# A decoder block in fp32 products: four pairs instead of three by seven products in three down groups of each FFN

## The chip, the core and the metric

The kernel runs on one core of one Trainium2 chip. The metric is the device time of the whole program in microseconds. The engines are named as the profile names them: PE is the matrix engine and PEld its weight loads, DVE the vector engine, ACT the scalar engine, POOL the GpSimd engine, SP the engine that issues most DMAs.

## What is computed

One layer of a hybrid decoder block on 256 tokens of width 2048: a half-step SwiGLU FFN, a mixer (gated DeltaNet beside stick-breaking attention), a second half-step FFN and an input embedding. The change touches the two FFNs:

```python
def swiglu(x, w_gu, w_down):
    gate, up = jnp.split(x @ w_gu, 2, axis=-1)
    return (jax.nn.silu(gate) * up) @ w_down
...
h = h + 0.5 * swiglu(rms_norm(h, ffn1_norm[i]), ffn1_w_gu[i], ffn1_w_down[i])
```

The hidden width is 5632, eleven blocks of 512.

## The kernel before

**Splits.** Every float32 matrix is split into a rounded part and its residue (`hi`, `lo`). A product of two such matrices takes three matmuls of 128 x 128 by 128 x 512: hi by hi, hi by lo and lo by hi. ACT makes `hi` with a copy that rounds, DVE makes `lo` with a subtraction.

**Pairs and groups.** Weights come in *pairs*: 256 rows by 512 columns, of 0.5 MB. `weight_pair` (L66 to L79) loads one on SP's queue into one of four `raw` tiles and splits it (L77 on ACT, L78 on DVE). A *group* makes four banks of the accumulator memory (PSUM): two column blocks `b` by two token halves. A gate/up group makes one block of gate and one of up. A down group makes two column blocks of the result; `nb` is 0 for a part's first down group and 2 for its second. A pair taken *plain* (L541 to L552) costs 12 matmuls for one column block.

**Parts.** The eleven hidden blocks are made in three parts, `PARTS` = (0 to 2), (3 to 6), (7 to 10). Within a part come the gate/up groups of its blocks, then the two down groups, which use those blocks as the left side.

**Seven products.** The first `ns` pairs of a group aren't taken plain. Seen over both column blocks and both row halves of a pair, they are a 2 by 2 product of blocks, done with seven products instead of eight (Winograd's form of Strassen's scheme). `NS` is 4 for gate/up groups. `NS_DOWN` is 2 in part one and 3 in parts two and three. One product is 3 x `ns` matmuls (`product`, L321 to L352). In the order `SEVEN` = 0, 1, 2, 4, 3, 5, 6, products 0, 4 and 6 use blocks of the left side as they are (A11, A12 and A22), the others use sums of them, the *left sides* `Sh` and `Sl`.

**The right sides.** The four quarters of the weights (row half by column block) are loaded whole into four R tiles (L279), for most groups on POOL's queue. `all_sums` (L289 to L327) makes the seven right sides one after the other: a copy that rounds on ACT (`shi`, L298) and a residue on DVE (`slo`, L299), each in two buffers. Between them a quarter is changed in place. `add` does it on DVE (L307). `add_loaded` does it with an accumulating DMA from POOL's queue, which reads the second operand from HBM again (L314). Before the change B11 + B12, right after the first product's right side, is an `add`; B12 + B22 and the last sum are `add_loaded`.

**Who comes when.** `plan` (L355) writes the order out by hand. While a group's plain pairs run, the seven products of the *next* group (its follower) are put between them: `at` says behind which plain pair. The first three quarters of the group after that are loaded behind products five to seven, the last one behind the first plain pair of the group that follows. `next_weights` (L88) makes pairs and right sides up to two or three ahead of use. A scheduler then orders each engine's instructions by this sequence and by what it expects to be ready. `tc.keep_in_program_order` pins one instruction to the place where it was written.

**Left sides.** `halves` (L423) makes them: DVE adds hi and lo back together (L456), forms four sums in place (L462), ACT rounds (L464), DVE takes the residue (L465). For the down groups of parts two and three it is started behind the sixth product of the part's last gate/up group (L536 to L539), with `at_once` = 1, one pair at a time. It runs as a *lane*: `lanes.step` after every plain pair takes it one `yield` further. The scheduler needs `Sh` free, of which there is one buffer.

**From gate/up to down.** `down_input` (L479) is a lane too. DVE multiplies (L482) and transposes in blocks (`tb`, L487), four DMAs write to HBM (`scr`, L493), one DMA reads back (`tT`, L498), and some steps later ACT and DVE split the block into `hTh` and `hTl` (L504, L505). `tb` and `tT` share one buffer. For a part's last block the DMAs go by SP's queue and the split stands `last` steps behind `tT`'s DMA: 3 for parts of four blocks, 2 for part one. `Group` sorts a first down group's plain pairs so that those of the last block come last.

**The tag `nat`** is a ring of four tiles of 128 x 512 floats. The copies `part` of partial products (L349) use it, and so do the left-side tiles here.

## Time and profile before

| | us |
|---|---|
| device time, median of 3 runs | 1944.5 (1944.01 to 1945.11) |
| the profiled execution | 1945.28 |
| its span in the profile | 1943.6 |
| FFN one, part two: last gate/up group, first and second down group | 341.0 to 377.2, to 418.7, to 464.9 |
| the other three places of the same kind begin near | 587, 1484 and 1730 |

The profile's times count from the start of the span. A line such as `L299 DVE TENSOR_TENSOR slo<-R,shi 128x1536 ...` names the line of the kernel, the engine, the operation, output and inputs, then count, total busy time and mean length in ns, then the time for which that engine was idle just before, and what ended it. A row of windows gives start and end, the length, and then for PE, PEld, DVE, ACT and POOL the busy time with the number of instructions, the granted PE clock, the DMA engines' share and GB/s. A row of the timeline gives start and length in us. In a row of waits stand the total, the number and the longest. Matmuls are pipelined: one begins before the one before it ends, so their lengths add up to more than the time they take.

### The profile page before, as it was taken

The page shows a single profiled execution, that of the slowest core. Times are in us where ns is not written, and L with a number is a line of the kernel's source. Part 1 is how long each engine was busy: PE and PEld are TensorE (multiplying, and loading weights), DVE is VectorE, ACT ScalarE, POOL GpSimd, SP SyncE. Part 2 cuts the span into 40 slices and gives each one's busy share as a digit, 9 for nine tenths or more (in the row PEclk, how much of TensorE's full clock was granted, in tenths as well). Part 3 has the DMA queues.
Part 4 walks back from the last instruction along what each step waited for, and adds up shares of the span by engine and source line. Part 5 has one row for each costly group of instructions (what it writes and reads, how often), then busy time and mean ns, then how long its engine had stood idle before and what let it go on. Part 6 is the DMA issues. An engine that isn't in the chain of part 4 may idle for free.

```text
span 1943.6 us, 24163 instructions
## 1 busy us (share of the span) xinstructions
PE 1928.1 (99%) x8884; PEld 1594.0 (82%) x8884; DVE 1570.4 (81%) x1703; ACT 1164.1 (60%) x1362; POOL 148.4 (8%) x226
## 2 busy tenths in 40 slices
PE   9999999999999999999999999999999999999998
PEld 7888888888888888878788888888888888888886
DVE  7879878997789766797856579899888987888865
ACT  6656666666666557664555456566556755657654
POOL 0010110000010000010100000010000100001000
PEclk9999999999999999999999999999999999999999
DMA  8778898888888765556565776788888987989764
GB/s 307 269 236 282 252 293 285 237 288 249 280 285 242 228 218 171 176 169 211 161 213 159 244 283 231 226 281 289 248 275 241 327 264 244 271 237 314 234 214 143
DMA packets 144182, 475.05 MB, mean 244 GB/s; under 512 B 19648, under 2 KB 47296, under 8 KB 129856
## 3 DMA queue, kind: packets, MB, share of 16 engines
q1 hardware_dynamic: 107200, 302.16, 44.4%
q0 software_dynamic: 25920, 160.44, 30.2%
q10 hardware_dynamic: 10944, 10.91, 1.8%
q8 instruction: 69, 1.13, 0.2%
q14 instruction: 49, 0.40, 0.1%
HBM read 451.44 MB, written 22.02 MB: 244 GB/s over the span
## 4 chain that ended last, share of the span: by engine, by line
PE 92%; DVE 5%; DMA 2%; issue 1%; ACT 0%; POOL 0%; SPq 0%; POOLq 0%; DVEq 0%; ACTq 0%
PE d L550 5%; PE d L552 5%; PE d L551 5%; PE u L551 5%; PE u L552 5%; PE u L550 5%; PE g L343 5%; PE g L342 5%; PE g L344 5%; PE g L551 4%; PE g L552 4%; PE pj L112 4%; PE pj L113 4%; PE pj L114 4%; PE g L550 4%; PE d L344 3%
## 5 line engine op out<-in xcount | busy, mean ns | idle before, releaser
L77 ACT CAST whi<-raw 128x1024 fp32r<-128x1024 f32 (+1 forms) x489 | 511.3, 1049 | 401.1 <-PE pj L114 106.6
L78 DVE TENSOR_TENSOR wlo<-raw,whi 128x1024 fp32r<-128x1024 f32 (+1 forms) x489 | 592.0, 1218 | 162.9 <-ACT whi L77 161.8
L299 DVE TENSOR_TENSOR slo<-R,shi 128x2048 fp32r<-128x2048 f32 (+2 forms) x224 | 444.9, 1989 | 132.1 <-ACT shi L298 130.1
L298 ACT CAST shi<-R 128x2048 fp32r<-128x2048 f32 (+2 forms) x224 | 373.9, 1671 | 141.5 <-DVE R L307 62.7
L112 PE MATMUL pj<-whi,nTh 128*128 128x512 f32 x448 | 179.4, 401 | 0.0
L113 PE MATMUL pj<-wlo,nTh 128*128 128x512 f32 x448 | 175.2, 391 | 1.1 <-DVE wlo L78 1.1
L114 PE MATMUL pj<-whi,nTl 128*128 128x512 f32 x448 | 174.9, 390 | 0.0
L550 PE MATMUL d<-whi,hTh 128*128 128x512 f32 x448 | 174.5, 390 | 0.0
L551 PE MATMUL d<-wlo,hTh 128*128 128x512 f32 x448 | 174.4, 389 | 0.0
L552 PE MATMUL d<-whi,hTl 128*128 128x512 f32 x448 | 173.4, 389 | 0.0
L551 PE MATMUL g<-wlo,nTh 128*128 128x512 f32 x400 | 156.6, 391 | 0.6 <-DVE wlo L78 0.6
L552 PE MATMUL g<-whi,nTl 128*128 128x512 f32 x400 | 156.0, 390 | 0.0
L551 PE MATMUL u<-wlo,nTh 128*128 128x512 f32 x400 | 155.8, 389 | 0.2 <-DVE wlo L78 0.2
L552 PE MATMUL u<-whi,nTl 128*128 128x512 f32 x400 | 155.6, 389 | 0.0
L550 PE MATMUL g<-whi,nTh 128*128 128x512 f32 x400 | 155.0, 391 | 0.6 <-ACT nTh L161 0.6
L550 PE MATMUL u<-whi,nTh 128*128 128x512 f32 x400 | 153.4, 389 | 0.0
L307 DVE TENSOR_TENSOR R<-R 128x2048 f32<-128x2048 f32 (+2 forms) x68 | 135.7, 1996 | 0.1
L113 PEld LDWEIGHTS pj<-wlo,nTh 128*128 128x128 f32 x448 | 84.2, 188 | 18.9 <-DVE wlo L78 2.7
L550 PEld LDWEIGHTS d<-whi,hTh 128*128 128x128 f32 x448 | 84.1, 188 | 18.1 <-ACT hTh L504 1.0
L552 PEld LDWEIGHTS d<-whi,hTl 128*128 128x128 f32 x448 | 84.1, 188 | 17.8
L114 PEld LDWEIGHTS pj<-whi,nTl 128*128 128x128 f32 x448 | 84.1, 188 | 17.6
L551 PEld LDWEIGHTS d<-wlo,hTh 128*128 128x128 f32 x448 | 84.1, 188 | 17.4
(332 smaller groups left out, 3447.0 us busy)
## 6 DMA issues: line engine op xcount, KB each, us to landing
raw<-in_w_gu SPq DMA_DIRECT2D x199, 512.0 KB, 5.8
raw<-in_w_down SPq DMA_DIRECT2D x112, 512.0 KB, 6.4
raw<-in_w_in SPq DMA_DIRECT2D x112, 512.0 KB, 3.4
R<-in_w_gu2q POOLq DMA_DIRECT2D x54, 1024.0 KB, 8.6
R<-in_w_gu1q POOLq DMA_DIRECT2D x48, 1024.0 KB, 8.3
raw<-in_w_out SPq DMA_DIRECT2D x32, 512.0 KB, 4.3
tT<-scr SPq DMA_DIRECT2D x22, 512.0 KB, 5.8
R<-in_w_down11q POOLq DMA_DIRECT2D x12, 768.0 KB, 7.0
```

The lines of the kernel that those rows point to most:

```text
L77: nc.scalar.copy(hi[:, j, :], raw[:, j, :])
L78: nc.vector.tensor_tensor(out=lo[:, j, :], in0=raw[:, j, :], in1=hi[:, j, :], op=ALU.subtract)
L112: nc.tensor.matmul(outs[t], xh[:, c], whi[:, j, :], start=st, stop=False)
L113: nc.tensor.matmul(outs[t], xh[:, c], wlo[:, j, :], start=False, stop=False)
L114: nc.tensor.matmul(outs[t], xl[:, c], whi[:, j, :], start=False, stop=sp)
L298: keep(nc.scalar.copy(hi, w))
L299: nc.vector.tensor_tensor(out=lo, in0=w, in1=hi, op=ALU.subtract)
L307: keep(nc.vector.tensor_tensor(out=self.raw[x], in0=self.raw[x], in1=self.raw[y], op=ALU.add))
L344: nc.tensor.matmul(out, xl, whi[:, g, :], start=False, stop=sp, skip_group_check=True)
L550: nc.tensor.matmul(out, xh[:, c], whi[:, j, :], start=st, stop=False, skip_group_check=True)
L551: nc.tensor.matmul(out, xh[:, c], wlo[:, j, :], start=False, stop=False, skip_group_check=True)
L552: nc.tensor.matmul(out, xl[:, c], whi[:, j, :], start=False, stop=sp, skip_group_check=True)
```

## The change

Per FFN, part two's two down groups and part three's first one take four pairs by seven products instead of three, and two plain pairs fewer each. For the first down group of parts two and three the order of products is `SEVEN_DOWN`: product 4 (A12 by B21, whose left side needs no sums) comes second, and B11 + B12 is made by an accumulating DMA. The left sides' sums for the first two pairs are formed one group earlier (`first_sides`), rounded as soon as `Sh` is free, and those for the third and fourth pair are formed from `tT`, the block before it is split. `last` becomes 2 where four pairs are taken.

```diff
-NS_DOWN = tuple(3 if i1 - i0 == 4 else 2 for i0, i1 in PARTS)
+NS_DOWN = (2, 2), (4, 4), (4, 3)
 SEVEN = (0, 1, 2, 4, 3, 5, 6)
+SEVEN_DOWN = (0, 4, 1, 2, 3, 5, 6)
...
+            self.seven = SEVEN_DOWN if kind == "dn" and part and nb == 0 else SEVEN
...
-            for i in SEVEN:
+            for i in self.seven:
                 ws = halved(*((0, 0), (0, 0), (0, 0), (0, 1), (1, 0), (1, 1), (0, 0))[i])
                 if i == 0:
-                    add((0, 0), (0, 1))
+                    (add if self.seven is SEVEN else add_loaded)((0, 0), (0, 1))
                     add_loaded((0, 1), (1, 1))
...
-                src = [sources(f"w_down{n}{p}", nb + b) for b in range(2)]
-                groups.append(Group("dn", p, [x[0] for x in src], [x[1] for x in src], NS_DOWN[p], len(groups) % 2, nb))
+                src = [sources(f"w_down{n}{p}{nb // 2}", b) for b in range(2)]
+                groups.append(Group("dn", p, [x[0] for x in src], [x[1] for x in src], NS_DOWN[p][nb // 2],
+                                    len(groups) % 2, nb))
...
-    def halves(kind, his, los, ns, wait=0, at_once=2):
+    def left_sides(kind, his, los):
...
+    def split_sums(s, g0, x, keep=lambda ins: ins):
+        n = x.shape[1] // NB
+        hi, lo = (y[:, g0:g0 + n].rearrange("p g j t y -> p (g j t y)") for y in s)
+        keep(nc.scalar.copy(hi, x))
+        keep(nc.vector.tensor_tensor(out=lo, in0=x, in1=hi, op=ALU.subtract))
+    def add_sides(x, src, keep=lambda ins: ins):
+        a11, a12, a21, a22 = x
+        b11, b12, b21, b22 = src
+        for o, y, z, op in ((a22, b21, b22, ALU.subtract), (a21, b11, b21, ALU.subtract),
+                            (a11, a22, b11, ALU.subtract), (a12, a11, b12, ALU.add)):
+            keep(nc.vector.tensor_tensor(out=o, in0=y, in1=z, op=op))
+    def sum_sides(x, his, los, g0):
+        n = x.shape[1] // NB
+        k0 = 2 * (g0 % 2)
+        hi, lo = (y[g0 // 2][:, k0:k0 + 2 * n].bitcast(F32).rearrange("p k x -> p (k x)") for y in (his, los))
+        nc.vector.tensor_tensor(out=x, in0=hi, in1=lo, op=ALU.add)
+        xv = x.rearrange("p (g j t y) -> p g j t y", g=n, j=2, t=2)
+        xs = [xv[:, :, j, t, :] for t in range(2) for j in range(2)]
+        add_sides(xs, xs)
...
+            def first_sides(p0):
+                for _ in range(4):
+                    yield
+                for g in range(2):
+                    x = act.tile([P, NB], F32, tag="nat", name="S", bufs=4)
+                    sum_sides(x, hTh[p0:], hTl[p0:], g)
+                    early.append(x)
+                    yield
+            def later_sides(s, made):
+                for g, x in made:
+                    yield
+                    split_sums(s, g, x, tc.keep_in_program_order)
...
                     keep(nc.vector.tensor_tensor(out=lo, in0=tv, in1=hi, op=ALU.subtract))
+                if pending:
+                    s, ns = pending.pop()
+                    made = []
+                    for g in range(2, ns):
+                        x = act.tile([P, NB], F32, tag="nat", name="S", bufs=4)
+                        xv = x.rearrange("p (j t q y) -> p j t q y", j=2, t=2, q=4)
+                        k = 2 * (g - 2)
+                        add_sides([xv[:, j, t] for t in range(2) for j in range(2)],
+                                  [tT[:, :, t, 32 * (k + j):32 * (k + j) + 32] for t in range(2) for j in range(2)],
+                                  keep)
+                        made.append((g, x))
+                    lanes.add(1, later_sides(s, made))
...
+                elif not dn and group.part and group.follower.kind == "gu" and group.follower.follower.kind == "dn":
+                    lanes.add(1, first_sides(i0))
...
-                        follower.product(SEVEN[one])
+                        follower.product(follower.seven[one])
                         if group.part and not dn and one == 5 and follower.kind == "gu" and \
                                 follower.follower.kind == "dn":
                             p = PARTS[group.part][0]
-                            lanes.add(1, halves("dn", Later(hTh, p), Later(hTl, p), NS_DOWN[group.part], 0, 1))
+                            lanes.finish(1)
+                            s = left_sides("dn", Later(hTh, p), Later(hTl, p))
+                            for g in range(2):
+                                split_sums(s, g, early.pop(0))
+                            pending.append((s, NS_DOWN[group.part][0]))
...
-                        last = (3 if i1 - i0 == 4 else 2) if len(hTh) == i1 else 0
+                        last = (6 - NS_DOWN[group.part][0] if i1 - i0 == 4 else 2) if len(hTh) == i1 else 0
```

The host side (`_layout`) packs the down weights per column half to match. The loops that took the left sides one pair at a time leave `halves`, which keeps two pairs at once for the other groups.

## The prediction

> **What bounds the kernel now.** I read the page's busy times first, then windows cut at the group borders of FFN one's part two, then the matrix engine's timeline, and last the waits and the vector engine's order at the places that the change touches.

> ```profile
> span 1943.6 us, 24163 instructions
> ...
> PE 1928.1 (99%) x8884; PEld 1594.0 (82%) x8884; DVE 1570.4 (81%) x1703; ACT 1164.1 (60%) x1362; POOL 148.4 (8%) x226
> ...
> L550 PE MATMUL d<-whi,hTh 128*128 128x512 f32 x448 | 174.5, 390 | 0.0
> ```

> PE is the bound over the whole span. But 390 ns is the length of one pipelined matmul, not what one fewer saves. That is the distance between starts:

> ```profile
> 413.22 0.39 PE L550 MATMUL d<-whi,hTh 128*128 128x512 f32 x1
> ...
> 426.82 0.39 PE L342 MATMUL g<-shi,nTh 128*128 128x512 f32 x1
> ```

> Sixty starts (five plain pairs of twelve) lie between these two, so one matmul costs 13.60 / 60 = 0.2267 us, and a plain pair, or a product of four pairs, 12 x 0.2267 = 2.72 us. [...]

> The four groups around the change, in order: part two's last gate/up group but one, its last gate/up group, its first and its second down group.

> ```profile
> core 0: us, PE busy (x) PEld busy (x) DVE busy (x) ACT busy (x) POOL busy (x), PEclk, DMA share, GB/s
> 300.20:341.00 40.80, 40.80 (x182) 33.78 (x181) 35.46 (x29) 24.05 (x21) 3.95 (x6) 1.00 0.85 261
> 341.00:377.20 36.20, 36.20 (x161) 29.73 (x160) 32.69 (x41) 23.73 (x27) 3.96 (x6) 1.00 0.82 238
> 377.20:418.70 41.50, 41.50 (x185) 34.37 (x184) 39.69 (x38) 26.23 (x26) 4.84 (x7) 1.00 0.93 312
> 418.70:464.90 46.20, 46.20 (x204) 37.86 (x203) 40.20 (x33) 25.43 (x22) 3.08 (x5) 1.00 0.82 257
> ```

> PE never rests here. DVE is at 87 to 96%, so a change that saves PE time here leans on the second-busiest engine.

> **The change, part by part.** *Products for plain pairs.* A pair taken by both column blocks costs 24 matmuls plain and 7 x 3 = 21 by seven products. Per FFN three groups move one pair each, in both FFNs: 6 x 3 = 18 matmuls, 18 x 0.2267 = **-4.1 us**. (With 390 ns it would be 7.0, which is wrong.)

> *What DVE gets instead*, in part two:

> ```profile
> L78 DVE TENSOR_TENSOR wlo<-raw,whi 128x1024 fp32r<-128x1024 f32 x487 | 590.6, 1220 | 160.2 <-ACT whi L77 159.1
> L299 DVE TENSOR_TENSOR slo<-R,shi 128x2048 fp32r<-128x2048 f32 x133 | 304.4, 2290 | 112.7 <-ACT shi L298 111.9 <-DMA raw<-in_w_gu 0.6
> L299 DVE TENSOR_TENSOR slo<-R,shi 128x1536 fp32r<-128x1536 f32 x56 | 97.9, 1754 | 10.3 <-ACT shi L298 10.1
> L307 DVE TENSOR_TENSOR R<-R 128x2048 f32<-128x2048 f32 x42 | 95.7, 2280 | 0.1
> ...
> L456 DVE TENSOR_TENSOR S<-hTh,hTl x14: 684/687/1222, 119.3 to 1742.7; 128x512 f32<-128x512 f32 x12, 128x1024 f32<-128x1024 f32 x2
> ...
> L462 DVE TENSOR_TENSOR S<-S 128x128 f32<-128x128 f32 x48 | 12.9, 290 | 0.1
> L298 ACT CAST shi<-R 128x2048 fp32r<-128x2048 f32 x133 | 254.3, 1913 | 104.1 <-DVE R L307 53.7 <-PE g L344 27.2 <-PE u L344 21.2
> ```

> Four plain splits go (-4.9), fourteen residues grow from 1.754 to 2.290 (+7.5), four sums of 1.74 (the rows at 339.11 and 349.95 below) become three of 2.280 (-0.1, the fourth goes to a DMA). Left sides: now three at 0.69 + 4 x 0.29 + about 0.69 = 2.5; then four, two of them without the first sum, as they are formed from the unsplit tT (+1.2). So +3.7: 148.0 of 164.7 us becomes 151.7 of 163.3, 93%. It still fits; what counts is where.

> *The last gate/up group*, where the first down group's products begin. DVE's order there:

> ```profile
> 337.23 1.76 DVE L299 TENSOR_TENSOR slo<-R,shi 128x1536 fp32r<-128x1536 f32 x1 [0.50 <-ACT shi L298]
> 339.11 1.75 DVE L307 TENSOR_TENSOR R<-R 128x1536 f32<-128x1536 f32 x1
> 347.65 1.76 DVE L299 TENSOR_TENSOR slo<-R,shi 128x1536 fp32r<-128x1536 f32 x1
> 349.95 1.73 DVE L307 TENSOR_TENSOR R<-R 128x1536 f32<-128x1536 f32 x1
> ...
> 336.10:359.50 23.40, 23.40 (x105) 19.11 (x103) 22.24 (x33) 11.42 (x14) 1.76 (x2) 1.00 0.68 166
> ...
> PEld g L551 <- DVE wlo L78: 0.3, 1, 0.3
> ```

> Residue, sum, residue, sum: the first three products hang on one serial chain on DVE, full to 22.24 of 23.40 us, and PE's one wait between 341 and 377 (last row; the same row stands at the other three such places) is for a plain residue queued in it. Out of this stretch go the sum B11 + B12 (1.75), the forming of two left sides (3.7, to the group before, which has 5.3 us free) and one 0.69; into it come a fourth side (1.9) and three residues longer by 0.54. About 2.6 us come free: the wait goes, **4 x 0.3 = -1.2 us**.

> *The sum by DMA, A12 second.* POOL issues in order: the last quarter's load, then the sums, each 0.9 us of an engine that is busy 4 of 36.

> ```profile
> 346.40 0.39 PE L342 MATMUL d<-shi,hTh 128*128 128x512 f32 x1
> ...
> 335.29 0.54 POOL L279 DMA_DIRECT2D R<-in_w_down11q  x1 [4.93 <-DVE slo L299]
> 341.16 0.89 POOL L314 DMA_DIRECT2D R<-in_w_down11q  x1 [5.33 <-DVE S L462]
> ...
> R<-in_w_down11q POOLq DMA_DIRECT2D x1, 768.0 KB, 4.7
> ...
> R<-in_w_gu1q POOLq DMA_DIRECT2D x1, 1024.0 KB, 9.0
> ```

> A12 needs the quarter that loads last, at 335.3. At 768 KB it landed after 4.7 us; 1 MB takes between that and the 9.0 of a 1 MB sum by DMA (last row, issued at 417.7): at 340 to 344.3. A12's product starts one plain pair and one product after the first one's 346.4, at 351.8; cast and residue take 4.2, so it has until 347.6. Behind the waiting cast on ACT stand plain casts, and PE waits for those: bounds 0 and 1.7 us (9.0 + 4.2 against 11.5) each; nearest to the 4.7 row, I take 0. B11 + B12 is issued when the first residue is done, near 340, and lands by 350, with the second sum behind it. Its product comes third, at 357.3, so its cast may start at 353: 3 us spare. Next in line is one sum on DVE and the third residue: 2.3 + 1.9 + 2.3 = 6.5 us against 5.44 between products, so the spare shrinks to 2 and holds. Cost 0; gone the cover, 1 to 2 us each.

> *The tiles that are held longer.* The sides formed early sit in two of the four `nat` buffers until the gate/up products release Sh; the copies of partial products share these, one at a time, so a third stays free: 0, and some 0.6 us of ACT per copy if it did not. Two sums from tT, 8 x 0.29 = 2.3 us of DVE, hold its only buffer, so the next block's transposes and its tT come 2.3 us later:

> ```profile
> 358.92 0.51 SPq L498 DMA_DIRECT2D tT<-scr  x1
> ...
> tT<-scr SPq DMA_DIRECT2D x1, 512.0 KB, 8.5
> ```

> It landed at 367.4 and is wanted at the first down group's start, after 377: hidden.

> *The last hidden block.* With eight plain pairs instead of ten, the fifth pair of the first down group already needs it; the earlier `last` moves its casts up one pair.

> ```profile
> 375.14 0.39 PE L342 MATMUL d<-shi,hTh 128*128 128x512 f32 x1
> ...
> 375.61 0.75 DVE L482 SCALAR_TENSOR_TENSOR sil<-u,rstd,sil 128x512 f32<-128x512 f32 x1
> 376.40 1.76 DVE L299 TENSOR_TENSOR slo<-R,shi 128x1536 fp32r<-128x1536 f32 x1
> 378.74 1.75 DVE L307 TENSOR_TENSOR R<-R 128x1536 f32<-128x1536 f32 x1
> 398.06 1.13 ACT L504 CAST hTh<-tT 128x512 fp32r<-128x512 f32 x2
> ...
> 161.68 0.39 PE L342 MATMUL d<-shi,hTh 128*128 128x512 f32 x1
> 162.36 0.49 PE L550 MATMUL d<-whi,hTh 128*128 128x512 f32 x1
> ...
> PEld d L550 <- ACT hTh L504: 0.5, 2, 0.3
> ```

> From the first gating multiply (375.6) to the cast, by way of the transposes and two DMAs on SP's queue, 22.5 us pass. Up's last matmul is out when the product at 375.14 starts; from there PE will be at the fifth pair after four products and four pairs, 8 x 2.72 = 21.8 us, or 21.3 after the multiply. Part one has eight plain pairs already: there the A12 product is put ahead of the fifth pair (161.68 before 162.36), and 0.5 us of weight-load waits remain. Done here too, it leaves 24.0 against 23.1 for the first cast half. The residue and the sum in the chain grow by 0.54 and 0.53. Bounds: 0 and, without the product ahead, 22.5 + 0.6 + 1.1 - 21.3 = 2.9 each. I take 0.2, near part one's row: **4 x 0.2 = +0.8**.

> *Part two's second down group.* It also makes the next part's left sides.

> ```profile
> 412.90:439.50 26.60, 26.60 (x119) 21.77 (x118) 26.47 (x25) 12.93 (x12) 1.76 (x2) 1.00 0.77 219
> ```

> DVE is full for 26.5 us, and PE gets through on five plain pairs in a row, two of which now go: 5.44 us less of PE cover, 2 x 1.22 = 2.4 less of DVE work. Bounds 0 and 3.0 per FFN; PE lists no wait here today, so I stay near 0: **2 x 0.2 = +0.4**. Part three's second group keeps its form.

> Sum: -4.1 - 1.2 + 0.8 + 0.4 = -4.1 us. The profiled execution took 1945.28 (span 1943.6), 0.8 above the median of 1944.5; the terms are differences, so from the median: **1940.4 us**.

> **Rivals.** *A: DVE becomes the bound in part two's second down group.* For: the full row above; against: no PE wait there now. At its bound: 2 x 3.0 in place of 0.4, 1946.0; half of it, 1943.0.
> *B, the other side: the last hidden block comes late.* Place: fifth plain pair, four times. Price 2.9 each in place of 0.2: 1940.4 + 4 x 2.7 = 1951.2. It makes the kernel slower by 0.2% from 2.2 us each. For: 22.5 against 21.3; against: part one's order, and its small wait.
> *C: the DMA engines are shared.*

> ```profile
> 360.00:415.00 55.00, 55.00 (x244) 45.56 (x243) 50.40 (x47) 37.96 (x39) 6.15 (x10) 1.00 0.98 332
> ```

> The added sum is a 1 MB transfer per changed first group beside weight loads, and the DMA share is 0.98 in the 55 us after it. If the sum or A12's quarter lands so late that the spare is used up, 1 to 1.7 us each: 1944.4 to 1947.2. Against: it falls into the stretch at 0.68. [...]
> *D: the change isn't what it says:* the planner leaves the order as it was, A12's product after all; then the DMA sum stands in the chain, as C.

> **How the numbers follow.** Forecast 0.64 (1938.8 to 1942.0; the low end has no new wait, 1939.2, and 0.4 for small old ones gone besides), A 0.15 (1942 to 1946), B 0.07, C 0.11, D 0.03. The range takes in the lower two thirds of A and C's near end: 1938.8 to 1944.6; left out are a third of A, most of C, B and D, some 0.2. A run of this kernel tells 0.2%, 3.9 us, from no change: faster means under 1940.6, which lies inside the forecast. Faster 0.50 (most of the forecast), same 0.41 (its rest, most of A and C), slower 0.09 (B and the end of C).

> **What will show it.** Right: 798 matmuls of down products instead of 672, at 0.227 us; no PE wait for a plain residue in the last gate/up group; sum and A12's quarter landed before their casts. Wrong: PE waits on hTh at the fifth pair (B), on Sl or a plain residue early in the second down group (A), ACT on a DMA into R (C).

## The result, and the profile after

| | before | after |
|---|---|---|
| device time, median of 4 runs each | 1944.5 us (1944.0 to 1945.1) | 1955.5 us (1954.1 to 1959.3) |
| ratio of after to before | | 1.006, 95% interval 1.0047 to 1.0073 |
| the profiled execution | 1945.28, span 1943.6 | 1959.32, span 1957.6 |

The kernel became 11 us slower. The forecast was 1940.4, the range 1938.8 to 1944.6.

The head of the page after the change, span and busy times:

```profile
span 1957.6 us, 24097 instructions
...
PE 1932.4 (99%) x8866; PEld 1592.0 (81%) x8866; DVE 1579.7 (81%) x1703; ACT 1172.9 (60%) x1354; POOL 152.3 (8%) x230
```

PE has the 18 matmuls fewer that were forecast (8866 against 8884). Its busy time grew by 4.3 us all the same, and 9.7 us of the longer span are idle time of PE. The waits over the whole kernel (who waits for whom: total, number, longest) say where:

```profile
PE d L346 <- DVE Sl L448: 7.9, 4, 2.0
...
PE d L345 <- DVE slo L301: 1.0, 5, 0.3
...
ACT shi L300 <- DMA R<-in_w_down220q: 9.8, 2, 7.7
ACT shi L300 <- DMA R<-in_w_down110q: 9.4, 2, 7.5
ACT shi L300 <- DMA R<-in_w_down120q: 9.4, 2, 7.4
ACT shi L300 <- DMA R<-in_w_down210q: 2.5, 1, 2.5
```

Four stalls of 2 us, one for each changed first down group, and behind them ACT waiting up to 7.7 us for a quarter of the weights. (The last row is no exception: at the third place the quarter landed at 1496.2 and its cast began at 1496.3, but the view puts that wait down to PE.) It is the wait that rival C named ("ACT on a DMA into R"), at two to four times its price: the time is 15 us above the forecast, where C had 4.0 to 6.8. In FFN one's part two the chain begins on POOL (timeline: start, length, line, what the engine waited for before):

```profile
329.92 0.54 POOL L281 DMA_DIRECT2D R<-in_w_down110q  x1 [4.85 <-DVE S L456]
332.89 0.89 POOL L316 DMA_DIRECT2D R<-in_w_down110q  x1 [2.44 <-DMA R<-in_w_down110q]
336.44 0.56 POOL L281 DMA_DIRECT2D R<-in_w_down110q  x1 [2.65 <-ACT Sh L447]
342.53 0.88 POOL L316 DMA_DIRECT2D R<-in_w_down110q  x1 [5.54 <-issue]
```

L281 is a load, L316 an accumulating transfer. The order is third quarter, **a sum**, last quarter, the other sum. The first sum is B12 + B22. Before the change it had to wait until DVE's B11 + B12 had read B12. With B11 + B12 read from HBM by a transfer of its own, nothing holds B12 + B22 back, and the scheduler put it ahead of the last quarter. The DMA view of the issues at 332.89, 336.44 and 342.53 (KB each, us to landing):

```profile
R<-in_w_down110q POOLq DMA_DIRECT2D x1, 1024.0 KB, 11.3
...
R<-in_w_down110q POOLq DMA_DIRECT2D x1, 1024.0 KB, 11.5
...
R<-in_w_down110q POOLq DMA_DIRECT2D x1, 1024.0 KB, 11.6
```

The last quarter, which A12's product takes, landed at 336.44 + 11.5 = 347.9; it was forecast for 340 to 344.3. B11 + B12 landed at 342.53 + 11.6 = 354.1; it was forecast for 350. What followed on ACT, and on DVE:

```profile
348.04 1.91 ACT L300 CAST shi<-R 128x2048 fp32r<-128x2048 f32 x1 [7.50 <-DMA R<-in_w_down110q]
...
354.21 1.91 ACT L300 CAST shi<-R 128x2048 fp32r<-128x2048 f32 x1 [1.87 <-DMA R<-in_w_down110q]
...
356.02 0.62 ACT L447 CAST Sh<-S 128x512 fp32r<-128x512 f32 x1
```

```profile
356.15 2.29 DVE L301 TENSOR_TENSOR slo<-R,shi 128x2048 fp32r<-128x2048 f32 x1 [1.33 <-ACT shi L300]
...
359.50 2.29 DVE L309 TENSOR_TENSOR R<-R 128x2048 f32<-128x2048 f32 x1
361.70 0.68 DVE L448 TENSOR_TENSOR Sl<-S,Sh 128x512 fp32r<-128x512 f32 x1
...
363.44 0.69 DVE L448 TENSOR_TENSOR Sl<-S,Sh 128x512 fp32r<-128x512 f32 x1
```

On ACT, `Sh` of the third pair (356.02) stands behind the cast that waits for the sum (354.21). On DVE, `Sl` stands behind the residue of that cast and the next sum. PE needs `Sl` and stands idle until 364.18. In this chain it is the landing of the sum that counts: the late quarter's own cast and residue are done by 352.3, before the sum's cast begins. PE's timeline:

```profile
361.81 0.39 PE L595 MATMUL u<-wlo,nTh 128*128 128x512 f32 x1
364.18 0.50 PE L346 MATMUL d<-shi,Sl 128*128 128x512 f32 x1 [1.98 <-DVE Sl L448]
...
365.01 0.63 PE L346 MATMUL d<-shi,Sl 128*128 128x512 f32 x1
365.44 0.63 PE L596 MATMUL u<-whi,nTl 128*128 128x512 f32 x1
```

The last two rows show a second cost. From 365.0 a matmul starts every 0.43 us instead of every 0.227. Windows of this stretch, and of the stretches behind the second and the fourth stall (the figure behind POOL's is the granted clock):

```profile
363.00:365.00 2.00, 0.82 (x3) 0.67 (x4) 2.00 (x3) 1.96 (x3) 0.00 (x0) 0.99 0.12 33
365.00:368.50 3.50, 3.50 (x10) 2.74 (x9) 1.73 (x2) 2.82 (x3) 0.90 (x1) 0.52 1.01 309
...
614.00:619.00 5.00, 4.28 (x19) 3.53 (x20) 3.47 (x4) 4.55 (x6) 0.88 (x1) 1.00 0.81 230
1763.00:1769.00 6.00, 6.00 (x19) 4.77 (x20) 4.49 (x3) 5.04 (x6) 0.87 (x1) 0.72 0.91 233
```

For 3.41 us the granted clock is half, behind the first and the fourth stall; behind the second (614) and the third (1512 to 1518) it is 1.00. Eight matmuls take the time of fifteen there, so each such stretch costs 7 x 0.2267 = 1.6 us.

**The sum for the profiled execution.** This execution is the slowest of the four. Its last matmul starts 13.8 us later than before. Comparing the same matmuls in both traces, ahead of and behind the changed groups of each FFN, puts 7.0 us of that into FFN one and 7.7 into FFN two, 14.7 together. The 0.8 us that come back lie near the end, outside the change: the profile before has a wait there (at 1921) that this one has not.

```profile
PE gt L125 <- DVE wlo L78: 0.5, 1, 0.5
```

Inside these stretches the matmuls that went give -4.1. Each of the four stalls costs 2.37 - 0.23 = 2.14 us by the rows above and 0.1 at the next start, together 9.0. Two stretches at half clock are 3.2. The rest comes from the distances of matmul starts: 3.6 in smaller waits of the same products, and 3.1 later on, in part two's and part three's first down groups (residues and the last hidden block). Waits of before that went give -0.6. That makes 14.2 of the 14.7; what is left is in differences too small to count one by one.

### The profile page after: what moved, and what is told of

Its sections match the earlier page's. It is cut to its first block, busy times and chain, and to the rows that moved or that the text cites. A ratio compares the mean times of both kernels' runs of the same rounds, so it can differ in the third digit from the quotient of the medians.

```text
span 1957.6 us, 24097 instructions
## 1 busy us (share of the span) xinstructions
PE 1932.4 (99%) x8866; PEld 1592.0 (81%) x8866; DVE 1579.7 (81%) x1703; ACT 1172.9 (60%) x1354; POOL 152.3 (8%) x230
## 3 DMA queue, kind: packets, MB, share of 16 engines
q8 instruction: 69, 1.13, 0.2%
## 4 chain that ended last, share of the span: by engine, by line
PE 85%; DVE 7%; DMA 4%; issue 2%; ACT 1%; POOL 0%; SPq 0%; DVEq 0%; POOLq 0%; ACTq 0%
PE u L596 4%; PE u L595 4%; PE u L594 4%; PE d L594 4%; PE g L345 4%; PE g L344 4%; PE g L346 4%; PE d L596 4%; PE d L595 4%; PE pj L113 4%; PE pj L114 4%; PE pj L115 4%; PE g L595 3%; PE g L596 3%; PE g L594 3%
## 5 line engine op out<-in xcount | busy, mean ns | idle before, releaser
L78 ACT CAST whi<-raw 128x1024 fp32r<-128x1024 f32 (+1 forms) x477 | 499.9, 1052 | 380.0 <-PE pj L115 109.1
L79 DVE TENSOR_TENSOR wlo<-raw,whi 128x1024 fp32r<-128x1024 f32 (+1 forms) x477 | 578.5, 1218 | 161.5 <-ACT whi L78 160.4
L301 DVE TENSOR_TENSOR slo<-R,shi 128x2048 fp32r<-128x2048 f32 (+2 forms) x224 | 467.5, 2089 | 138.5 <-ACT shi L300 135.9
L300 ACT CAST shi<-R 128x2048 fp32r<-128x2048 f32 (+2 forms) x224 | 392.5, 1754 | 184.4 <-DVE R L309 80.9
L594 PE MATMUL d<-whi,hTh 128*128 128x512 f32 x400 | 156.1, 391 | 0.3 <-ACT hTh L530 0.3
L595 PE MATMUL d<-wlo,hTh 128*128 128x512 f32 x400 | 155.4, 389 | 0.0
L596 PE MATMUL d<-whi,hTl 128*128 128x512 f32 x400 | 155.1, 390 | 0.0
L113 PEld LDWEIGHTS pj<-whi,nTh 128*128 128x128 f32 x448 | 84.2, 188 | 16.6
L345 PE MATMUL g<-slo,nTh 128*128 128x512 f32 x234 | 91.4, 390 | 0.0
L346 PE MATMUL g<-shi,nTl 128*128 128x512 f32 x234 | 91.1, 390 | 0.0
## 6 DMA issues: line engine op xcount, KB each, us to landing
raw<-in_w_gu SPq DMA_DIRECT2D x199, 512.0 KB, 6.4
raw<-in_w_in SPq DMA_DIRECT2D x112, 512.0 KB, 3.4
R<-in_w_gu2q POOLq DMA_DIRECT2D x54, 1024.0 KB, 8.4
raw<-in_w_down SPq DMA_DIRECT2D x100, 512.0 KB, 6.3
R<-in_w_gu1q POOLq DMA_DIRECT2D x48, 1024.0 KB, 8.2
raw<-in_w_out SPq DMA_DIRECT2D x32, 512.0 KB, 4.4
tT<-scr SPq DMA_DIRECT2D x22, 512.0 KB, 4.9
```

The lines of the kernel that those rows point to most:

```text
L78: nc.scalar.copy(hi[:, j, :], raw[:, j, :])
L79: nc.vector.tensor_tensor(out=lo[:, j, :], in0=raw[:, j, :], in1=hi[:, j, :], op=ALU.subtract)
L113: nc.tensor.matmul(outs[t], xh[:, c], whi[:, j, :], start=st, stop=False)
L300: keep(nc.scalar.copy(hi, w))
L301: nc.vector.tensor_tensor(out=lo, in0=w, in1=hi, op=ALU.subtract)
L345: nc.tensor.matmul(out, xh, wlo[:, g, :], start=False, stop=False, skip_group_check=True)
```

## The experiments

The first theory, "DMA": three transfers of 1 MB are in flight at once, A12's quarter and the sum land late, and all else follows. Its rival, "order": the left sides of the third and fourth pair stand too late in ACT's and DVE's order, whatever lands when. Later runs ask where the expected 4 us stay when the stalls are gone. Each ratio is against runs of the kernel before that were taken beside it.

### B11 + B12 on DVE again

```diff
                 if i == 0:
-                    (add if self.seven is SEVEN else add_loaded)((0, 0), (0, 1))
+                    add((0, 0), (0, 1))
                     add_loaded((0, 1), (1, 1))
```

> The changed kernel with one part undone: B11 + B12 is a sum on DVE again, in all groups. Theory DMA (the DMA of B12 + B22, which no longer waits for anything on DVE, is issued ahead of the last quarter's load; two sums and the quarter share the DMA engines, the quarter and B11 + B12 land 11.5 us after issue, ACT waits 9.4 us per place for R, and Sh, Sl and PE wait behind it): the quarter lands within 9 us, ACT's waits for R fall under 3 us per place, PE's four waits for Sl (2.0 us each) go, 1939 to 1944 us. Theory order (Sl of the third and fourth pair is late because DVE has it behind a residue, a plain residue and a sum, whatever the DMAs do): DVE has 2.3 us more ahead of it, PE's waits for Sl are 2 us or longer, 1955 to 1960 us.

Measured: 1944.2 us, ratio 0.9997 (0.9988 to 1.0007). The DVE sum brings the old order on POOL back, and the last quarter landed after 5.1 us instead of 11.5, at the same size and place. The DMA view of that issue (at 336.58), and the waits:

```profile
R<-in_w_down110q POOLq DMA_DIRECT2D x1, 1024.0 KB, 5.1
```

```profile
PE d L344 <- ACT part L352: 0.9, 4, 0.2
...
ACT shi L300 <- DMA R<-in_w_down110q: 1.0, 1, 1.0
```

No wait for `Sl`, and no half clock in the FFNs: the mean granted clock of the profiled execution is 0.999 as before the change, against 0.997 in the changed kernel. One line of the change carries all 11 us of the loss. The 4 us that the matmuls should bring are missing, though: the time is just above the first theory's 1939 to 1944.

### Both sums by DMA, B12 + B22 pinned behind B11 + B12

```diff
-            def add_loaded(x, y):
+            def add_loaded(x, y, pin=False):
...
-                nc.gpsimd.dma_start(out=self.raw[x], in_=self.quarters[y[1]][y[0]], accum_op=ALU.add)
+                ins = nc.gpsimd.dma_start(out=self.raw[x], in_=self.quarters[y[1]][y[0]], accum_op=ALU.add)
+                if pin:
+                    tc.keep_in_program_order(ins)
...
-                    add_loaded((0, 1), (1, 1))
+                    add_loaded((0, 1), (1, 1), self.seven is not SEVEN)
```

> The changed kernel, with the DMA of B12 + B22 kept behind the last quarter's load and behind the DMA of B11 + B12 on POOL. Theory DMA: the quarter lands within 9 us and B11 + B12 within 10 us of issue, ACT's waits for R fall to 3 us or less per place, PE's waits for Sl to under 0.5 us each, 1940 to 1946 us. Theory order: no gain, 1953 to 1957 us.

Measured: 1943.6 us, ratio 0.9996 (0.9987 to 1.0005). POOL's timeline, and the DMA view for the issues at 335.48 and 341.58:

```profile
335.48 0.54 POOL L281 DMA_DIRECT2D R<-in_w_down110q  x1 [5.98 <-ACT Sh L449]
341.58 1.79 POOL L316 DMA_DIRECT2D R<-in_w_down110q  x2 [5.56 <-issue]
```

```profile
R<-in_w_down110q POOLq DMA_DIRECT2D x1, 1024.0 KB, 5.1
...
R<-in_w_down110q POOLq DMA_DIRECT2D x1, 1024.0 KB, 8.0
```

The quarter goes out first and lands after 5.1 us, the sum after 8.0. These are the 340 to 344 and the 350 of the prediction. B12 + B22, issued right behind, is now the slow one with 14.5 us; it is wanted later. The same cast and the same `Sl` as above, here on ACT's and DVE's timeline:

```profile
349.70 1.91 ACT L300 CAST shi<-R 128x2048 fp32r<-128x2048 f32 x1 [0.67 <-DVE wlo L79]
...
358.93 0.68 DVE L450 TENSOR_TENSOR Sl<-S,Sh 128x512 fp32r<-128x512 f32 x1
```

From the start of the cast to that of the fourth pair's `Sl` 9.23 us pass, exactly as in the changed kernel (354.21 to 363.44). The order of that work is the same; only the landing of the sum differs. So the sum by DMA as such does no harm; the transfer that slipped ahead of the last quarter, and so delayed the sum too, does. What is left are waits at the other end, on the last hidden block, both of them at the third place:

```profile
PE d L596 <- ACT hTh L532: 1.0, 1, 1.0
PE d L598 <- DVE hTl L533: 0.7, 1, 0.7
```

### The changed kernel with three pairs as before

```diff
-NS_DOWN = (2, 2), (4, 4), (4, 3)
+NS_DOWN = (2, 2), (3, 3), (3, 3)
```

> The changed kernel with the groups of three pairs as before (NS_DOWN = (2, 2), (3, 3), (3, 3)): A12 second, the sum B11 + B12 by DMA and the early left sides stay, the 18 matmuls come back, the quarters are 768 KB again. POOL still issues the sum B12 + B22 ahead of the last quarter. Theory 'size' (three transfers of 1 MB are what lands late): each lands after 0.75 x 11.5 = 8.6 us, the last quarter some 3 us sooner and more than the stall of 2.1 us, so PE's wait for Sl goes: time 1942 to 1945, no half clock. Rival 'order' (a third transfer ahead of the last quarter is late at any size): ACT still waits 5 us or more per place for R and PE 1 to 2 us per place for Sl: 1948 to 1953.

Measured: 1943.9 us, ratio 0.9996 (0.9987 to 1.0005). POOL's order is the bad one, in the timeline, and the DMA view has for these two issues:

```profile
330.55 0.89 POOL L316 DMA_DIRECT2D R<-in_w_down110q  x1 [0.53 <-DVE wlo L79]
336.00 0.55 POOL L281 DMA_DIRECT2D R<-in_w_down110q  x1 [4.57 <-ACT Sh L447]
```

```profile
R<-in_w_down110q POOLq DMA_DIRECT2D x1, 768.0 KB, 9.4
...
R<-in_w_down110q POOLq DMA_DIRECT2D x1, 768.0 KB, 6.8
```

The quarter landed at 342.8, 5 us sooner than with 1 MB, and PE has no wait on `Sl` or `slo` in these groups. So the overtaking did no harm here at 768 KB and cost 11 us at 1 MB. With three pairs the casts and residues are shorter too (1.48 and 1.75 us against 1.91 and 2.29), so this run alone doesn't part the transfers' size from the engines'; the two runs above do, at full size.

### A12's product fourth, with the sum by DMA; and the left sides sooner

```diff
-SEVEN_DOWN = (0, 4, 1, 2, 3, 5, 6)
+SEVEN_DOWN = [0, 1, 2, 4, 3, 5, 6]
```

> The changed kernel with A12's product fourth again, B11 + B12 still by DMA. The second product then needs the DMA's sum at 351.8 us where it landed at 354.1 in the changed kernel. Theory DMA: ACT waits for that sum instead of the last quarter, PE waits 4 us or more per place, 1958 to 1970 us. Theory order: as the changed kernel or a little better, 1950 to 1957 us.

Measured: 1982.5 us, ratio 1.0197 (1.0182 to 1.0212). Now the sum that lands at 354 is wanted second, and PE waits for its cast:

```profile
PE d L344 <- ACT shi L300: 17.2, 8, 4.0
```

To these come stretches at half clock at all four places, 10.2 us at the first and 6.8 at the others: nine times 3.41 us, some 14 us at 1.6 each (mean granted clock 0.991). The theory had counted waits alone, and its upper end of 1970 was missed by 12. The second edit leaves the order of products and rounds the third and fourth pair's sides right behind their sums:

```diff
                 for g, x in made:
-                    yield
                     split_sums(s, g, x, tc.keep_in_program_order)
+                yield
```

> The changed kernel with the third and fourth pair's left sides rounded right after their sums, without a step between; on DVE this puts Sl ahead of the third product's residue and the sum behind it, and on ACT Sh ahead of the third product's cast. The DMAs are as in the changed kernel. Theory DMA: ACT still waits 9.4 us per place for R; PE now waits for the third product's residue or what comes behind it, 1 to 2 us per place, 1946 to 1955 us. Theory order: PE's waits at these places go, 1939 to 1944 us.

Measured: 1956.2 us, ratio 1.0056 (1.0039 to 1.0072), as slow as the changed kernel and 1 us over the first theory's range. `Sl` is there at 356, and PE waits for the residue behind it instead, 8.5 us in ten pieces (mean granted clock 0.998):

```profile
PE d L345 <- DVE slo L301: 8.5, 10, 1.2
...
ACT shi L300 <- DMA R<-in_w_down110q: 8.8, 3, 7.1
```

The wait for R stays, and only the last to come has changed. With that the rival "order" falls.

### What the other parts of the change are worth

Three runs start from the kernel with B11 + B12 on DVE (1944.2), where the landing is no question. First, A12's product fourth (the edit of the section before):

> B11 + B12 on DVE again and A12's product fourth, as before the change; the four pairs and the early sides stay. Theory 'A12 second gives DVE room': the second product then needs residue, sum, residue on DVE and all four left sides by 352 instead of 357; PE waits 1 to 4 us at each of four places for Sh, Sl or slo: 1948 to 1960. Rival 'the order of products hardly matters once the sum is off the DMA': time 1943.5 to 1946.

Measured: 1951.6 us, ratio 1.0036 (1.0022 to 1.0049): 7 us more, in 4 waits of 1.6.

```profile
PE d L344 <- ACT shi L300: 6.1, 4, 1.6
```

Second, the left sides made as before the change, for four pairs (`one_by_one` is a loop like the old one):

```diff
...
-                    lanes.add(1, first_sides(i0))
+                    pass
...
-                            lanes.finish(1)
-                            s = left_sides("dn", Later(hTh, p), Later(hTl, p))
-                            for g in range(2):
-                                split_sums(s, g, early.pop(0))
-                            pending.append((s, NS_DOWN[group.part][0]))
+                            lanes.add(1, one_by_one("dn", Later(hTh, p), Later(hTl, p), NS_DOWN[group.part][0]))
```

> B11 + B12 on DVE again, and the left sides made as before the change (one pair at a time from hTh and hTl, started behind the sixth product; four pairs now). Four pairs by seven products and A12 second stay. Theory 'DVE's chain in the last gate/up group': 4 x 2.5 us of left sides stand in it again instead of some 6, PE waits 0.5 to 2 us at each of four places: 1946 to 1952. Rival 'the early sides bring nothing': PE's stalls within 0.2 us per place of those with the sum on DVE alone, time 1943.5 to 1945.

Measured: 1955.5 us, ratio 1.0057 (1.0042 to 1.0072): 11 us more, beyond the 1952 of the theory's upper end. Third, `Sl` earlier (the second edit of the section before):

> B11 + B12 on DVE again, and the left sides of the third and fourth pair rounded right behind their sums. With the sum on DVE alone the first of the products that use sums was interrupted while Sl of the third and fourth pair was late, its right side's buffer came free late, and PE lost 0.39 us at each of four places to a copy of a partial product. Theory 'Sl is the last to come': Sl comes ahead of the residue of the third product, these four stalls go, span 1942.6 - 1.6 = 1941.0, time 1942 to 1943. Rival 'DVE is full': the residue and the sum behind it are later by 1.4 us, PE waits for slo instead, 0.4 us or more at each of the four places: time 1944 or more.

Measured: 1945.2 us, ratio 1.0002 (0.9993 to 1.0011). The four waits for `part` stayed as they were, and new ones for `hTh` came:

```profile
PE d L344 <- ACT part L352: 0.9, 4, 0.2
PE d L594 <- ACT hTh L530: 0.7, 2, 0.6
```

So `Sl` was not the last to come: a miss of that theory. Its rival gave the time (1944 or more) but not the wait, as PE still waited for `part` at the four places and hardly for `slo`. A12 second and the early sides are worth 7 and 11 us to a kernel of four pairs. They pay for the four pairs; they bring nothing beyond.

### B12 + B22 on DVE, B11 + B12 by DMA

```diff
                 if i == 0:
                     (add if self.seven is SEVEN else add_loaded)((0, 0), (0, 1))
-                    add_loaded((0, 1), (1, 1))
+                    if self.seven is SEVEN:
+                        add_loaded((0, 1), (1, 1))
...
                     add_loaded((0, 0), (1, 0))
+                    if self.seven is not SEVEN:
+                        tc.keep_in_program_order(nc.vector.tensor_tensor(out=self.raw[0, 1], in0=self.raw[0, 1],
+                                                                         in1=self.raw[1, 1], op=ALU.add))
```

> The changed kernel with B12 + B22 made by DVE instead of by a DMA, pinned behind the residue of the fourth right side in the order of products; B11 + B12 stays a DMA. One accumulating DMA instead of two is in flight beside the last quarter's load. With both kept as DMAs in program order, PE lost 0.9 and 1.2 us at one of the four places to the last hidden block, behind a sum that landed 1.8 us later there. Theory 'what the four pairs lack is DMA time, and DVE has some 3 us idle between 363 and 380': no wait for Sl, no cast that waits over 2 us for R, hidden block 0.2 to 0.5 us per place: of the 4.1 us of matmuls some 2.5 to 3.5 remain, time 1941 to 1942, span 1939 to 1940.5. Rival 'DVE has no room either': the residues of the fifth to seventh right side and the gating multiply come 2.3 us later, PE waits 0.5 to 1 us per place for slo or hTh: time 1943.5 to 1946.

Measured: 1946.6 us, ratio 1.001 (1.0001 to 1.0019). The hoped-for 1941 is missed, and the time is even above the rival's 1946. No stall is left in the last gate/up group, but at all four places PE loses 0.55 to 0.6 us, by the distances of its starts, where the last hidden block is taken, and 0.2 at a cast before it in part two:

```profile
PEld d L348 <- ACT shi L300: 2.5, 6, 0.4
PEld d L598 <- ACT hTh L534: 2.3, 8, 0.3
```

The profiled execution took 1945.5 us, 1.1 less than the median, so these rows don't account for the whole time.

No version run here beats the kernel before by more than its interval. The best are the pinned sums and the three pairs, both at 0.9996. The traces say where the 4.1 us of the matmuls stayed. By the same matmuls ahead of and behind the changed groups, the two FFNs together are 0.5 us shorter than before with the sum on DVE, 0.4 shorter with B12 + B22 on DVE, and 0.3 longer with the transfer pinned. So waits inside the FFNs take back all or nearly all of it in each of the three.

### The half clock by itself

A kernel of PE bursts with gaps that a DVE subtraction sets:

```python
for n in GAPS:
    bank = ps.tile([P, NB], F32, tag="bank", name="bank", bufs=4)
    for i in range(48):
        c = slice(128 * (i % 2), 128 * (i % 2) + 128)
        nc.tensor.matmul(bank, s[:, c], moving, start=i == 0, stop=i == 47)
    keep(nc.vector.tensor_tensor(out=junk, in0=bank[:, 0:64], in1=zeros[:, 0:64], op=ALU.subtract))
    s = next_side(n)
```

> A kernel of its own: none of the block is computed. Eighty bursts of 48 matmuls (128x128 by 128x512, a weight load each), between them a gap that a DVE subtraction of 256 to 2560 columns sets, each size ten times, so that the gaps fall differently in the clock's windows of 3.41 us. In the changed kernel two of four equal stalls of 2.1 us were followed by 3.41 us at half clock, 410.0 windows apart, those of which one window was idle for over 57%. Theory 'share of a free-running window': gaps under some 1.9 us are never followed by half clock, gaps of 2.0 to 3.3 us in some of their ten repeats and not in others, by how they lie in the window, gaps over 3.7 us in nearly all; a half clock lasts a multiple of 3.413 us and its starts are whole windows apart. Rival 'only a gap longer than a window': no half clock at all behind gaps under 3.4 us.

Measured: gaps up to 1.93 us, from one matmul's start to the next, were never followed by half clock; of those of 2.19 us 5 of 10 were, of 2.46 none, of 3.00 5 of 10, of 3.53 4 of 9. The longest gap came out at 3.53 us, so what the theory said of gaps over 3.7 wasn't tested. The mean granted clock was 0.978. All starts of half clock are whole multiples of 3.413 us apart (8, 13, 62, 70, 75 ... times that from the first); the stretches between these boundaries are the windows below. The kernel's period fell into step with them, and each size met two positions only. The second probe lets the position drift (bursts of 61, thirty gaps of 2.19 us and thirty of 2.46):

> As p1: none of the block is computed. Thirty gaps of one size (1280 columns on DVE, 2.2 us) and thirty of the next (1536 columns, 2.5 us) between bursts of 61 matmuls, 13.8 us, so that each gap lies some 2.4 us further in the windows of 3.413 us than the one before. In p1 two positions per size came up only: at 2.2 us a window idle for 58% was followed by half clock and one of 38% wasn't, at 2.5 us one of 61% wasn't, three windows behind an earlier half clock. Theory 'the idle share of one window decides, near 55%': of the thirty gaps of 2.2 us about a quarter to a third (those with over 55% of one window: the gap less 0.23 us is 58% of a window at most, so only positions within some 0.1 to 0.3 us of fitting whole: 5 to 10), of those of 2.5 us 8 to 15, and no gap whose largest share is under 50%. Rival 'something else decides as well': gaps with equal shares come out both ways.

Measured: 5 of the 30 gaps near 2.2 us and 16 of the 29 of 2.46 us, one more than the range for these; the mean granted clock was 0.964. Two pairs of windows, each cut at the boundaries that the first half clock gives; both hold one gap of 2.46 us:

```profile
513.27:516.68 3.41, 1.44 (x7) 0.86 (x5) 1.89 (x2) 0.00 (x0) 0.00 (x0) 1.00 0.00 0
516.68:520.09 3.41, 3.31 (x8) 2.69 (x9) 0.00 (x0) 0.00 (x0) 0.00 (x0) 0.50 0.00 0
530.34:533.75 3.41, 2.10 (x10) 1.40 (x8) 1.27 (x2) 0.00 (x0) 0.00 (x0) 1.00 0.00 0
533.75:537.16 3.41, 2.64 (x12) 2.23 (x13) 0.62 (x1) 0.00 (x0) 0.00 (x0) 1.00 0.00 0
```

Where the gap falls into one window (PE busy 1.44 of 3.41), the next window is at half clock (0.50). Where it is split over two (2.10 and 2.64), the clock stays at 1.00. Counted from the end of one matmul's turn to the next start, in both probes all windows that one gap left idle for 63% or more were followed by half clock, and none of 57% or less was. Between these both happen: of the gaps that filled 58% of a window 5 of 5 were followed in the first probe and 5 of 13 in the second, and of the 7 in both probes that filled 60 to 62% none. So the rival has a point: between 57 and 63% equal shares came out both ways, and what else decides there stays open. Of the changed kernel's two stalls that were followed, the first fills 63% of its window; the fourth fills 57% by this count, and 60% with the smaller wait behind it. The two that were not followed are split over two windows and fill at most 46% and 36% of one.

## Why the prediction was wrong

- **The matmuls: right.** 798 matmuls of down products were forecast, and the row of each of the three kinds shows 152 + 114; 3 x 266 = 798. Each is worth 0.2267 us, -4.1 in all. But the kernel with the pinned sums keeps none of it. Its last matmul starts 1.7 us earlier than before, and that is gained outside the changed groups: 0.9 before the first of them and 0.8 at the wait near 1921. In the changed groups FFN one gained 1.2 us and FFN two lost 1.5.
- **"The sum by DMA, A12 second", cost 0: the step that failed.** It took POOL's order to be "the last quarter's load, then the sums". B12 + B22's only tie to that place was the DVE sum that the change removes. So the quarter did not land after some 5 us but after 11.5, and the sum B11 + B12 not by 350 but at 354.1. The prediction had left that sum 2 us to spare; 4.1 late less 2 is about the stall of 2.1. Its bounds of 0 and 1.7 us per place assumed one transfer too few and stopped at the plain casts behind a waiting cast. The chain ran on over the cast of the sum to `Sh`, `Sl` and PE. The runs with the sum on DVE and with the transfer pinned show that this is the whole loss.
- **Rival C, chance 0.11: right in the wait that it named, too small.** That sharing the DMA engines is what made the transfers late was an assumption of it and was not shown. Its upper end was 1947.2, 1.7 us per place. Measured are 2.25 per stall and 0.9 in smaller waits round it. It knew nothing of the clock, which added 1.6 us at two of the four places in the profiled execution. The changed kernel's spread of 5 us, against 1 before, may come from that; this wasn't tested. Rival D did not come: A12's product is second in the trace.
- **The last gate/up group, -1.2: the mechanism right, the size wrong.** The waits for a plain residue went, and with three pairs none is left. But the 0.3 us was the weight load's wait, and PE lost less. Its starts around 353.45 in the kernel before (0.25 and 0.34 us apart instead of 0.227 each):

```profile
353.45 0.50 PE L551 MATMUL g<-wlo,nTh 128*128 128x512 f32 x1
353.79 0.39 PE L552 MATMUL g<-whi,nTl 128*128 128x512 f32 x1
```

  That is 0.14 per place, 0.6 in all. In the kernel with three pairs both FFNs together are 0.7 us shorter than before, by the same matmuls in both traces, which is nearer to 0.6 than to 1.2.
- **"About 2.6 us of DVE come free": used up.** As soon as one sum returns to DVE, four waits for `part` or the hidden block come: there is no 2.3 us to spare, neither early in the chain (the sum on DVE: 0.5 us per place by the distances of starts) nor late in it (B12 + B22 on DVE).
- **The last hidden block, 4 x 0.2 = +0.8: too small.** 0.3 in part two and 0.6 in part three with the sum on DVE, 0.55 to 0.6 at all four with B12 + B22 on DVE. Rival B's 2.9 was not met; nearest to it is the third place with the transfer pinned, where PE lost 0.9 and 1.2 us to this block.
- **Part two's second down group, 2 x 0.2: nearly right.** In the group itself small waits of 0.25 us before are 0.15 after, and rival A falls. Its products' right sides, made while the first group runs, cost 0.4 to 0.45 us instead, at 404 in the changed kernel and at 398 with the transfer pinned.

## What to carry to other kernels

Removing an operation also removes the waits that it imposed on others. Before pricing a moved sum, list who was held back by the old one, because the scheduler may put a transfer that nothing holds back any more ahead of the one that is needed. A transfer time read from a trace holds for what is in flight and queued there: the same 1 MB took 5.1 us and 11.5 us at one place. Price a long stall of PE with the clock as well (here two of four stalls of 2.1 us were followed by 1.6 us of loss at half clock), and read what PE loses from the distances of its starts rather than from the waits of its weight loads (0.14 us against 0.3 at 353.45). When a version looks faster, see in which stretch the time was gained before crediting it to the change.

## What the hardware showed beyond that

**Accumulating transfers.** One of 1 MB took 8.3 us beside weight loads (B12 + B22 at 345.30, in the run with B11 + B12 on DVE). With a second one issued right behind it (both within the 1.79 us of POOL's row at 341.58), it took 8.0 and the second 14.5 (the pinned transfers). When two of them and a load of 1 MB followed each other within 10 us, they took 11.3 to 11.6, and the load between them 11.5 in place of 5.1; over all four places these range from 10.2 to 12.0. What makes the load so late, the bytes in flight or the way in which POOL's transfers share its queue, no run here tells apart.
